# Latent attention in a two-layer hybrid trunk: queries one pair of heads ahead, the key latent normed between the first two pairs' queries, a fourth group of transposes on another bank

## The chip, the cores and the metric

The kernel runs on one core of one Trainium2 chip. The metric is the device time of one execution in microseconds, as the median over several runs.

## The reference

Two layers of a decoder trunk work on 512 tokens of width 1024 in float32. Each layer norms its input, projects it, sends it through three branches side by side (a state-space branch "SSD", latent attention "MLA", a gated delta rule "GDN"), merges them by gates and ends with a feed-forward block. The change touches the attention branch only:

```python
def mla_mixer(cq, ckv, k_rope, cos, sin, q_norm_g, w_uq, kv_norm_g, w_ukv):
    # H = 8 heads; cq is 512 wide, ckv 256; per head 128 + 64 (rotary) query columns
    q = (rmsnorm(cq, q_norm_g) @ w_uq).reshape(Bsz, S, H, MLA_NOPE + MLA_ROPE)
    q_nope, q_pe = jnp.split(q, [MLA_NOPE], axis=-1)
    q_pe = apply_rope(q_pe, cos[:, :, None, :], sin[:, :, None, :])
    kv = (rmsnorm(ckv, kv_norm_g) @ w_ukv).reshape(Bsz, S, H, MLA_NOPE + MLA_V)
    k_nope, v = jnp.split(kv, [MLA_NOPE], axis=-1)
    k_pe = apply_rope(k_rope, cos, sin)          # one rotary key for all heads
    ...
    # per block of 128 queries, causal:
    sc = q_nope @ k_nope + q_pe @ k_pe
    pr = jax.nn.softmax(sc * scale, axis=-1)
    out = pr @ v
```

## The kernel before

**Products.** Every float32 operand is split into a high part rounded to the matmul's format and a low remainder: ScalarE makes the high part (names ending in "h", or "hi"), VectorE the low part ("l", "lo"). A product is three matmuls into one accumulator, high by high (L181), low by high (L182 or L183), high by low (helper mm3, L179). A weight block is fetched by a transfer on SP's queue into "wraw" (two buffers), then split into "whi" (L159, ScalarE) and "wlo" (L160, VectorE). TensorE's accumulators live in eight banks: four named "acc" for projections, three named "sm" for small products, transposes and scores, one named "yt" that collects an attention head's output.

**Order.** The program is written in one order, and a scheduler decides ahead of time how the instructions of each engine stand behind each other, from dependencies, from priorities (`tc.high_priority`) and from when a buffer of a pool comes free. On the chip each engine takes its own list in that order and waits on semaphores of the others. A transfer inside the chip's memory that ScalarE issues (queue ACTq) stands in ScalarE's list as well.

**Attention before.** The two latents are in token-major tiles. The function `latent` squares and sums each (ScalarE), takes the power -1/2 (POOL), scales the rows (L495, VectorE), transposes in groups of four 128x128 blocks (L500, TensorE) into a bank, and splits the result with the gain (L260 ScalarE, L261 VectorE) into cqh, cql (four tiles each) or ckh, ckl (two each). The query latent has four such groups, for which there are three "sm" banks. Both latents are normed before any query is made. Then a loop over the four pairs of heads (hp, L540) does, in this order: the pair's query weights and 36 query matmuls from cqh and cql (three accumulators of 4 x 3 matmuls), the copies qh and ql (L568, L569), the scaled rotary part qp (L575); its rotation `rope`, which swaps halves by four transfers on ScalarE's queue (L513) and combines them on VectorE (L515 to L517); a second swap by two transfers (L580) so that either head has its half on the partitions it needs; the copies qps (L584, L586) and qpl (L585). Then the pair's keys and values: weights, 2 x 6 key matmuls, kh and kl; four value accumulators and vh, vl. Then for each of the two heads the scores of four row blocks, each from six matmuls (L617 to L622), the maximum (L626), the exponential (L629), the scaling, transposes of the probabilities (L639) and the product with v (L655 to L657) in the "yt" bank. Behind pair 0 the step sizes of the recurrent branches are called (`step_sizes`, L375 to L416); the scheduler moves much of them forward.

The kernel's start norms the layer's input in the same manner: row tiles scaled on VectorE (L291, by nrs from POOL, L265), transposed (L296), split into xh and xl (L261); the first products are with a narrow weight block into "yt" (L181 to L183 with mix as weights).

## Time and profile before

| | |
|---|---|
| median of 3 runs | 2350.89 us (2350.47 to 2352.99) |
| profiled execution | 2350.16 us |
| its span | 2348.4 us |
| granted TensorE clock | 0.999 |
| TensorE busy | 2307.8 us |
| VectorE busy | 1607.3 us |
| ScalarE busy | 1154.4 us |
| POOL busy | 58.5 us |

The profile is of one execution. "Busy" is the time in which an engine worked; it does not tell who waited for whom. The attention stage is short beside the whole: in layer 0 it runs from about 55 us to about 215 us, in layer 1 from about 1215 us to about 1365 us, with projections of other branches mixed in.

### The profile page before, as it was taken

The numbers are of one execution on the slowest core, as the hardware profiler recorded it, in microseconds if no ns is written. First come the engines' busy times: TensorE is split into PE (matmuls) and PEld (weight loads), VectorE is DVE, ScalarE is ACT, GpSimd is POOL, SyncE is SP. The second block draws the span as 40 slices with busy tenths as digits, with TensorE's granted clock in tenths as the row PEclk, the third lists the DMA queues.
The fourth block names the chain that finished last, engine by engine and source line by source line (L and its number), as shares of the span: only waits on it lengthen the run. The fifth ranks groups of instructions, "written<-read, shape, count | busy, mean of one in ns | idle before, by whom it ended". The sixth has DMA issues, their size and how long they took to land.

```text
span 2348.4 us, 32069 instructions
## 1 busy us (share of the span) xinstructions
PE 2307.8 (98%) x11972; PEld 1896.2 (81%) x11972; DVE 1607.3 (68%) x3184; ACT 1154.4 (49%) x2305; POOL 58.5 (2%) x76
## 2 busy tenths in 40 slices
PE   8999999999999999999999999999999999999998
PEld 7787788888887888888887887888887878888886
DVE  6776756775675458767757777667766645677668
ACT  5655434533453345545656553444334534555545
POOL 0000000000000000000000000000000000000000
PEclk9999999999999999999999999999999999999999
DMA  4322232252222443233132222323422224333231
GB/s 131 91 64 72 65 97 70 79 149 73 73 63 72 143 150 102 72 125 117 46 100 78 73 72 70 93 65 106 117 81 66 62 81 161 126 111 105 90 108 45
DMA packets 194172, 215.16 MB, mean 92 GB/s; under 512 B 32352, under 2 KB 153696, under 8 KB 194016
## 3 DMA queue, kind: packets, MB, share of 16 engines
q1 hardware_dynamic: 190496, 207.87, 29.1%
q10 hardware_dynamic: 3520, 5.25, 0.9%
q8 instruction: 94, 1.54, 0.3%
q14 instruction: 62, 0.51, 0.1%
HBM read 200.50 MB, written 7.34 MB: 89 GB/s over the span
## 4 chain that ended last, share of the span: by engine, by line
PE 90%; DVE 5%; DMA 2%; ACT 1%; POOL 1%; issue 1%; SPq 0%; ACTq 0%; DVEq 0%; POOLq 0%
PE acc L181 23%; PE acc L182 23%; PE acc L183 23%; PE sm L183 2%; PE sm L181 2%; PE sm L182 2%; PE sm L735 1%; DVE wlo L160 1%; PE sm L639 1%; PE yt L182 1%; PE yt L181 1%; PE yt L183 1%; PE sm L1000 1%; PE sm L296 1%; PE sm L461 1%
## 5 line engine op out<-in xcount | busy, mean ns | idle before, releaser
L160 DVE TENSOR_TENSOR wlo<-wraw,whi 128x512 fp32r<-128x512 f32 x552 | 377.9, 688 | 401.8 <-ACT whi L159 391.8
L159 ACT CAST whi<-wraw 128x512 fp32r<-128x512 f32 x552 | 341.9, 621 | 623.6 <-PE acc L182 407.9
L181 PE MATMUL acc<-xh,whi 128*128 128x512 f32 (+1 forms) x1184 | 462.0, 391 | 0.0
L182 PE MATMUL acc<-xl,whi 128*128 128x512 f32 (+1 forms) x1184 | 459.4, 388 | 0.0
L183 PE MATMUL acc<-xh,wlo 128*128 128x512 f32 (+1 forms) x1184 | 459.0, 388 | 0.0
L182 PEld LDWEIGHTS acc<-xl,whi 128*128 128x128 f32 x1184 | 223.0, 188 | 42.5 <-issue 1.0
L183 PEld LDWEIGHTS acc<-xh,wlo 128*128 128x128 f32 x1184 | 222.9, 188 | 41.8 <-issue 0.5
L181 PEld LDWEIGHTS acc<-xh,whi 128*128 128x128 f32 x1184 | 222.8, 189 | 41.7 <-issue 0.5
L181 PE MATMUL acc<-yh,whi 128*128 128x512 f32 x384 | 153.1, 402 | 0.0
L182 PE MATMUL acc<-yl,whi 128*128 128x512 f32 x384 | 152.3, 397 | 0.0
L183 PE MATMUL acc<-yh,wlo 128*128 128x512 f32 x384 | 151.4, 394 | 0.0
L183 PE MATMUL acc<-whi,xl 128*128 128x512 f32 (+1 forms) x384 | 144.0, 375 | 0.0
L181 PE MATMUL acc<-whi,xh 128*128 128x512 f32 (+1 forms) x384 | 143.9, 376 | 0.0
L182 PE MATMUL acc<-wlo,xh 128*128 128x512 f32 (+1 forms) x384 | 143.4, 373 | 0.0
L676 DVE SCALAR_TENSOR_TENSOR cva<-acc,pc,cva 128x511 f32<-128x511 f32 (+2 forms) x168 | 120.2, 743 | 16.7 <-ACT cva L672 9.5
L159 ACT CAST whi<-wr 128x512 fp32r<-128x512 f32 x128 | 79.5, 621 | 68.3 <-PE acc L183 32.7
L181 PE MATMUL acc<-whi,yh 128*128 128x512 f32 x256 | 99.7, 390 | 0.0
L183 PE MATMUL acc<-whi,yl 128*128 128x512 f32 x256 | 99.7, 389 | 0.0
L182 PE MATMUL acc<-wlo,yh 128*128 128x512 f32 x256 | 99.6, 389 | 0.0
L160 DVE TENSOR_TENSOR wlo<-wr,whi 128x512 fp32r<-128x512 f32 x128 | 85.8, 685 | 12.6 <-ACT whi L159 12.1
L182 PEld LDWEIGHTS acc<-yl,whi 128*128 128x128 f32 x384 | 72.2, 188 | 16.1 <-issue 1.9
L181 PEld LDWEIGHTS acc<-yh,whi 128*128 128x128 f32 x384 | 71.6, 188 | 16.8 <-ACT yh L260 2.3
(409 smaller groups left out, 4597.9 us busy)
## 6 DMA issues: line engine op xcount, KB each, us to landing
wraw<-in_w_in_dram SPq DMA_DIRECT2D x148, 512.0 KB, 3.6
wraw<-in_w_up_dram SPq DMA_DIRECT2D x64, 512.0 KB, 3.7
wr<-in_w_down_dram SPq DMA_DIRECT2D x32, 1024.0 KB, 5.0
wraw<-in_w_mla_out_dram SPq DMA_DIRECT2D x16, 512.0 KB, 3.4
wraw<-in_w_ssd_out_dram SPq DMA_DIRECT2D x16, 512.0 KB, 3.4
wraw<-in_w_gdn_out_dram SPq DMA_DIRECT2D x16, 512.0 KB, 3.3
wraw<-in_w_out_dram SPq DMA_DIRECT2D x16, 512.0 KB, 3.7
wraw<-in_mla_w_uq_dram SPq DMA_DIRECT2D x16, 384.0 KB, 3.4
```

Source lines behind the costliest of these rows:

```text
L159: act.copy(hi, raw)
L160: dve.tensor_tensor(lo, raw, f32(hi), ALU.subtract)
L181: pe.matmul(o, ah, bh, start=start, stop=False, skip_group_check=more)
L182: pe.matmul(o, ah, bl, start=False, stop=False, skip_group_check=more)
L183: pe.matmul(o, al, bh, start=False, stop=stop, skip_group_check=more)
L296: pe.transpose(ps[:, j * P : (j + 1) * P], xr[j % 2][:, kk * P : (kk + 1) * P], ident)
L461: pe.matmul(ps, w, cum[1][:, t].rearrange("p i l -> p (i l)"), start=True, stop=True)
L639: pe.transpose(ps[:, n : n + P], pn[t][:, kb * P : (kb + 1) * P], ident)
L676: dve.scalar_tensor_tensor(acc[:, d:], ps[:, : S - d], taps_[3 - d], acc[:, d:], ALU.mult, ALU.add)
L735: pe.matmul(py[:, h * 64 : (h + 1) * 64], e2[h // 4][:, h % 4, :], xd[:, h * 64 : (h + 1) * 64], start=True, stop=True)
L1000: pe.matmul(po[:, h * P : (h + 1) * P], pt_[:, h, :], vn[:, h * P : (h + 1) * P], start=True, stop=True)
```

## The change

It has three parts. (1) In `latent`, the fourth group of transposes (k == 3, query latent only) is written to the "yt" bank instead of an "sm" bank. (2) The loop's body is cut into three functions, `queries(hp)`, `keys(hp)` and `attend(hp, ...)`. The order is now: queries of pair 0, norm of the key latent, queries of pair 1; then for each pair its keys and values, its scores and output, and behind pairs 0 and 1 the queries of the pair after next. (3) Since two pairs' queries are alive at once, the odd pairs' qh, ql, qps and qpl lie in tiles that others use later (the output tiles "y", two of the query latent's tiles), and the half of qpl that must be zero is cleared anew on POOL (`clean`, eight memsets more). The lines of the loop move: the swap transfers L513 and L580 of before are L512 and L585 after, the qps copies L584 and L586 are L594 and L596, the scores L617 to L622 are L634 to L639, qh is written in L548 and qp in L580.

```diff
@@ latent
             for k in range(nk):
-                ps = sm_bank()
+                ps = y_bank() if k == 3 else sm_bank()
@@
         cqh, cql = latent(cq_tok, 512, g_q, "cq")
-        ckh, ckl = latent(ck_tok, 256, g_kv, "ck")
...
-        qpl = [mk(ml, [P, S], F32R, f"qpl{j}") for j in range(2)]
+        base_qpl = [mk(ml, [P, S], F32R, f"qpl{j}") for j in range(2)]
+        clean = lambda x, j: pool.memset(f32(x[64 * (1 - j) : 64 * (1 - j) + 64]), 0.0)
         for j in range(2):
-            pool.memset(f32(qpl[j][64 * (1 - j) : 64 * (1 - j) + 64]), 0.0)
+            clean(base_qpl[j], j)
...
-        for hp in range(4):
+        y_home = lambda k: [mk(lp, [P, S], F32R, f"y{e}{k}") for e in "hl"]
+        cq_home = lambda k: [mk(ml, [P, S], F32R, f"cq{e}{k}") for e in "hl"]
+        def queries(hp):
...
-            qs = head_tiles(pq, "q", scale)
+            qs = head_tiles(pq, "q", scale, [y_home(hp * 2 + j if hp == 1 else 6 + j) for j in range(2)] if hp % 2 else None)
...
-            qps = [mk(ml, [P, S], F32R, f"qps{j}") for j in range(2)]
+            if hp % 2:
+                qps, qpl = zip(*((y_home if hp == 1 else cq_home)(k) for k in ((4, 5) if hp == 1 else (2, 3))))
+                for j in range(2):
+                    clean(qpl[j], j)
+            else:
+                qps, qpl = [mk(ml, [P, S], F32R, f"qps{j}") for j in range(2)], base_qpl
...
+            return qs, qps, qpl
+        def keys(hp):
...
+            return ks, vs
+        def attend(hp, qs, qps, qpl, ks, vs):
...
+        qq = [queries(0)]
+        ckh, ckl = latent(ck_tok, 256, g_kv, "ck")
+        qq.append(queries(1))
+        for hp in range(4):
+            attend(hp, *qq[hp], *keys(hp))
+            if hp < 2:
+                qq.append(queries(hp + 2))
             if hp == 0:
                 dec, ndec, beta, dtq, dsk, g24 = step_sizes()
```

How the instructions stand on the engines moves at three places of layer 0. The first is TensorE's list where the query latent's last transposes meet the first query matmuls; "ct" is the identity, "mix" the scaled latent, acc_725 to acc_727 the three accumulators of pair 0. Before:

```order
L500 MATMUL sm_652<-ct_75,mix_224 128x128
L181 MATMUL acc_725<-cqh_120_630,whi_730 128x512
L181 MATMUL acc_726<-cqh_120_630,whi_730 128x512
L181 MATMUL acc_727<-cqh_120_630,whi_730 128x512
L500 MATMUL sm_659<-ct_75,mix_221 128x128
L500 MATMUL sm_659<-ct_75,mix_222 128x128
L500 MATMUL sm_659<-ct_75,mix_223 128x128
L500 MATMUL sm_659<-ct_75,mix_224 128x128
L182 MATMUL acc_725<-cql_124_634,whi_730 128x512
```

The same place in the changed kernel, where pair 0's accumulators are acc_691 to acc_693:

```order
L500 MATMUL sm_652<-ct_75,mix_224 128x128
L500 MATMUL yt_659<-ct_75,mix_221 128x128
L500 MATMUL yt_659<-ct_75,mix_222 128x128
L500 MATMUL yt_659<-ct_75,mix_223 128x128
L500 MATMUL yt_659<-ct_75,mix_224 128x128
L181 MATMUL acc_691<-cqh_120_630,whi_696 128x512
L181 MATMUL acc_692<-cqh_120_630,whi_696 128x512
L182 MATMUL acc_691<-cql_124_634,whi_696 128x512
```

The transposes have moved ahead of all query matmuls, and two query matmuls instead of three now stand ahead of the first one that reads cql.

The second place is ScalarE's list around the copies kh of pair 0's keys. Before:

```order
L568 ACTIVATE qh_792<-acc_725 128x512
L568 ACTIVATE qh_796<-acc_726 128x512
L552 CAST whi_1140<-wraw_1138 128x256
L553 CAST whi_1140<-wraw_1138 128x128
L552 CAST whi_1155<-wraw_1138 128x256
L256 CAST kh_846<-acc_832 128x512
L553 CAST whi_1155<-wraw_1138 128x128
L575 ACTIVATE qp_800<-acc_727 128x512
L513 DMA mix_802<-qp_800 32x512
L256 CAST kh_850<-acc_833 128x512
```

In the changed kernel mix_773 is pair 0's rotated part, mix_777 its swapped form, whi_925 and whi_929 the key weights, acc_822 the first query accumulator of pair 1:

```order
L585 DMA mix_777<-mix_773 64x512 x2
L594 CAST qps_162_780<-mix_773 64x512
L159 CAST whi_925<-wraw_923 128x512
L159 CAST whi_929<-wraw_923 128x512
L594 CAST qps_163_781<-mix_773 64x512
L596 CAST qps_162_780<-mix_777 64x512
L596 CAST qps_163_781<-mix_777 64x512
L256 CAST kh_947<-acc_933 128x512
L548 ACTIVATE yh_189_889<-acc_822 128x512
```

kh stood ahead of pair 0's swap transfers and now stands behind them and behind the four qps copies. On TensorE the readers of kh follow the first key accumulator at once (acc_934 is the second):

```order
L183 MATMUL acc_933<-ckh_171_805,wlo_930 128x512
L634 MATMUL sm_1003<-kh_947,qh_758 128x256
L634 MATMUL sm_1017<-kh_947,qh_758 128x256
L634 MATMUL sm_1031<-kh_947,qh_758 128x384
L181 MATMUL acc_934<-ckh_170_804,whi_925 128x512
```

Before, the second key accumulator and value matmuls stood between the first key accumulator and the first score matmul; now nothing does.

The third place is VectorE's list at the program's start; nrs_279 is the norm factor of the fourth row tile, xr_283 that tile scaled, xl_31 the first low part of the normed input. Before:

```order
L264 TENSOR_SCALAR nrs_279<-nrs_279 128x1
L261 SCALAR_TENSOR_TENSOR xl_31_130<-sm_150,pc_104,xh_23_122 128x256
L261 SCALAR_TENSOR_TENSOR xl_33_132<-sm_159,pc_104,xh_25_124 128x256
L160 TENSOR_TENSOR mix_189<-wraw_186,mix_188 128x384
L261 SCALAR_TENSOR_TENSOR xl_32_131<-sm_150,pc_104,xh_24_123 128x256
L160 TENSOR_TENSOR mix_193<-wraw_186,mix_192 128x384
```

In the changed kernel:

```order
L264 TENSOR_SCALAR nrs_279<-nrs_279 128x1
L291 TENSOR_SCALAR xr_283<-h_89,nrs_279 128x1024
L160 TENSOR_TENSOR mix_189<-wraw_186,mix_188 128x384
L261 SCALAR_TENSOR_TENSOR xl_31_130<-sm_150,pc_104,xh_23_122 128x256
L160 TENSOR_TENSOR mix_193<-wraw_186,mix_192 128x384
L261 SCALAR_TENSOR_TENSOR xl_33_132<-sm_159,pc_104,xh_25_124 128x256
```

The scaling of the fourth row tile and one weight subtraction have moved ahead of the first xl.

More of the change, by code (lines that the diff above doesn't have):

```diff
@@ L532, in hybrid_kernel, with head_tiles @@
             pool.memset(f32(x[:, :P]), 0.0)
-        qpl = [mk(ml, [P, S], F32R, f"qpl{j}") for j in range(2)]
+        base_qpl = [mk(ml, [P, S], F32R, f"qpl{j}") for j in range(2)]
+        clean = lambda x, j: pool.memset(f32(x[64 * (1 - j) : 64 * (1 - j) + 64]), 0.0)
         for j in range(2):
-            pool.memset(f32(qpl[j][64 * (1 - j) : 64 * (1 - j) + 64]), 0.0)
+            clean(base_qpl[j], j)
         scale = (128 + 64) ** -0.5
         yh, yl = [None] * KD, [None] * KD
-        for hp in range(4):
+        def head_tiles(pss, nm, c=None, homes=None):
+            res = []
+            for j, ps in enumerate(pss):
+                hi, lo = homes[j] if homes else (mk(ml, [P, S], F32R, nm + e, 3) for e in "hl")
+                if c is None:
+                    split_act(hi, lo, ps)
+                else:
+                    act.mul(hi, ps, c)
+                    dve.scalar_tensor_tensor(lo, ps, c, f32(hi), ALU.mult, ALU.subtract)
+                res.append((hi, lo))
+            return res
+        y_home = lambda k: [mk(lp, [P, S], F32R, f"y{e}{k}") for e in "hl"]
+        cq_home = lambda k: [mk(ml, [P, S], F32R, f"cq{e}{k}") for e in "hl"]
+        def queries(hp):
             def q_weights():
@@ L558, in hybrid_kernel @@
             *pq, pp = dense_F(q_weights(), tiles(384), 512, cqh, cql)
-            def head_tiles(pss, nm, c=None):
-                res = []
-                for ps in pss:
-                    hi = mk(ml, [P, S], F32R, nm + "h", 3)
-                    lo = mk(ml, [P, S], F32R, nm + "l", 3)
-                    if c is None:
-                        split_act(hi, lo, ps)
-                    else:
-                        act.mul(hi, ps, c)
-                        dve.scalar_tensor_tensor(lo, ps, c, f32(hi), ALU.mult, ALU.subtract)
-                    res.append((hi, lo))
-                return res
-            qs = head_tiles(pq, "q", scale)
+            qs = head_tiles(pq, "q", scale, [y_home(hp * 2 + j if hp == 1 else 6 + j) for j in range(2)] if hp % 2 else None)
             qp = mk(ml, [P, S], F32, "qp")
@@ L580, in hybrid_kernel @@
                 act.dma_start(qd[64 * i : 64 * i + 64], qr[64 * (1 - i) : 64 * (1 - i) + 64])
-            qps = [mk(ml, [P, S], F32R, f"qps{j}") for j in range(2)]
+            if hp % 2:
+                qps, qpl = zip(*((y_home if hp == 1 else cq_home)(k) for k in ((4, 5) if hp == 1 else (2, 3))))
+                for j in range(2):
+                    clean(qpl[j], j)
+            else:
+                qps, qpl = [mk(ml, [P, S], F32R, f"qps{j}") for j in range(2)], base_qpl
             for j in range(2):
```

## The prediction

> **What bounds the kernel now.** I read the page first, for the span, the engines' shares and the chain that ended last. Row by row these are the span, the busy times and the chain by engine:

> ```profile
> span 2348.4 us, 32069 instructions
> PE 2307.8 (98%) x11972; PEld 1896.2 (81%) x11972; DVE 1607.3 (68%) x3184; ACT 1154.4 (49%) x2305; POOL 58.5 (2%) x76
> PE 90%; DVE 5%; DMA 2%; ACT 1%; POOL 1%; issue 1%; SPq 0%; ACTq 0%; DVEq 0%; POOLq 0%
> ```

> TensorE is busy for 98% of the span and is on the chain for 90% of it. The change leaves the number of TensorE's operations as it is, so only the time in which TensorE stands still can change. I therefore asked next for TensorE's waits (engine, waiting line, releaser: total us, times, longest):

> ```profile
> PE sm L620 <- ACT qps L586: 3.2, 3, 1.9
> PE acc L181 <- DVE vl L257: 2.2, 3, 0.8
> PE sm L500 <- DVE mix L495: 1.9, 2, 1.0
> PE sm L500 <- DVE cql L261: 1.2, 1, 1.2
> PE acc L181 <- ACT cqh L260: 0.6, 2, 0.3
> PE yt L656 <- DVE mix L257: 0.4, 2, 0.2
> ```

> These six are all of the attention stage, over both layers, and they add up to 9.5 us, 0.4% of the span. That is the most visible idle time that the change can take away. Everything that decides is therefore a matter of a microsecond at a place, and I went on to the timeline, TensorE's rows (start, duration, operation, in brackets the idle time before and its releaser):

> ```profile
> 60.24 0.98 PE L181 MATMUL acc<-cqh,whi 128*128 128x512 f32 x3 [0.29 <-ACT cqh L260]
> 62.43 0.66 PE L500 MATMUL sm<-ct,mix 128*128 128x128 f32 x4 [1.21 <-DVE cql L261]
> 66.36 0.63 PE L500 MATMUL sm<-ct,mix 128*128 128x128 f32 x4 [0.95 <-DVE mix L495]
> 80.19 0.47 PE L181 MATMUL acc<-cqh,whi 128*128 128x512 f32 x1 [0.65 <-DVE vl L257]
> 80.49 0.40 PE L182 MATMUL acc<-cql,whi 128*128 128x512 f32 x1
> 80.72 0.39 PE L183 MATMUL acc<-cqh,wlo 128*128 128x512 f32 x1
> 147.49 0.38 PE L620 MATMUL sm<-kps,qps 128*128 128x256 f32 x1 [0.78 <-ACT qps L586]
> 1278.83 0.39 PE L620 MATMUL sm<-kps,qps 128*128 128x256 f32 x1 [1.85 <-ACT qps L586]
> ```

> The second row is the query latent's last group of transposes, the third the key latent's first; the pair 80.49 and 80.72 gives what a 512-column matmul costs when it does not wait, 0.23 us from start to start. A difference of 0.2% (4.7 us) is about what a measurement of this kernel can tell from no change.

> **Part one, the transposes and the latents.** Before, the fourth group of transposes (62.43) waits for the first "sm" bank, which VectorE's cql copy empties. In the new order it writes the free "yt" bank and runs straight behind the third group. But the three query matmuls that stood ahead of it need cqh alone, and now only two of them do so before the first one that reads cql. VectorE's rows there:

> ```profile
> 61.01 0.26 DVE L402 SCALAR_TENSOR_TENSOR g<-spl,aexp 128x96 f32<-128x96 f32 x1
> 61.63 2.06 DVE L261 SCALAR_TENSOR_TENSOR cql<-sm,pc,cqh 128x512 fp32r<-128x512 f32 x3
> ```

> VectorE has the step-size chain of the recurrent branch ahead of cql until 61.6 and writes the first cql about 62.3 (a third of the 2.06 us that three take, behind 61.63). TensorE reaches it at about 61.1: the wait of 1.21 comes back as one of about 1.2 on the next matmul in layer 0. What is gained there is the four transposes moved into the hole, 4 x 0.11 us (0.63 for four with the tail of the last), say 0.35. In layer 1 that wait does not exist before (the row above has 1 time). The key latent's wait for L495 (0.95 in layer 0, 1.9 over both) goes: its transposes now stand behind 36 query matmuls, 36 x 0.23 = 8.3 us, and the squares, POOL's power and the scaling lie below that cover. If the cover were gone it would cost the 0.95 again. Gain: 1.9 + 2 x 0.35 = **2.6 us**, bounds 1.9 and 3.7 (all of L495, cql and cqh).

> **Part two, queries one pair ahead.** Pairs 1 and 2 no longer wait for qps (3.2), since their rotary halves are made one pair earlier; the accumulators that waited for the vl copies (2.2) now follow other work; and the two yt waits (0.4) have queries standing between. Gain **5.8 us**, bounds 3 and 5.8.

> What is late next is the first pair. In the new order three score matmuls of pair 0 stand right behind the first key accumulator, and on ScalarE the copy kh that they read stands behind both swap transfers of pair 0, four qps copies and two weight casts. Two of the qps copies wait for the swap to land. Before, kh stood ahead of all that. ScalarE's rows of before (ACTq is its sequencer issuing a transfer):

> ```profile
> 74.78 0.60 ACT L575 ACTIVATE qp<-acc 128x512 f32<-128x512 f32 x1
> 75.41 0.51 ACTq L513 DMA_DIRECT2D mix<-qp  x1
> 75.97 0.59 ACT L256 CAST kh<-acc 128x512 fp32r<-128x512 f32 x1 [0.59 <-PE acc L183]
> 81.78 0.50 ACTq L580 DMA_DIRECT2D mix<-mix  x1
> 82.76 0.54 ACTq L580 DMA_DIRECT2D mix<-mix  x1
> 85.62 1.27 ACT L586 CAST qps<-mix 64x512 fp32r<-64x512 f32 x2
> ```

> From qp to the first swap transfer is 81.78 - 74.78 = 7.0 us, and nothing in between is taken away. In the new order qp's last matmul is the 36th behind 62.3, so qp comes at about 70.7, and the swaps go out at about 77.7 and 78.3. How long a swap takes, from the view of line L580 and from the transfers issued between 111.7 and 112.3 us:

> ```profile
> DMA to landing us min/median/max: 2.2/2.3/5.6
> wraw<-in_mla_w_uq_dram SPq DMA_DIRECT2D x1, 384.0 KB, 3.9
> mix<-mix ACTq DMA_DIRECT2D x2, 128.0 KB, 3.3
> ```

> Alone it lands in 2.3 us; beside a weight load the two of 111 us average 3.3, and the slowest takes 5.6. Alone: landed 80.6, two copies of 1.27 together 81.9, kh 0.6 more, 82.5. TensorE gets there after 36 query matmuls, 8 transposes, 36 more query matmuls and 6 key matmuls: 62.3 + 78 x 0.23 + 8 x 0.11 = 81.1. So the wait is 1.2 to 1.4; with a landing of 4.3, 2.0 us longer. The weight load of pair 2 is released by pair 1's casts, at about the same 77.7, so the meeting is possible, not certain. I take 1.2, ends 0 and 4.5 (a landing of 5.6).

> Behind it, the second key accumulator takes the bank of pair 1's first query, which is emptied by a ScalarE copy right behind kh and a VectorE subtraction: 82.5 + 0.6 + 0.6 = 83.7 against 82.8 for TensorE (kh plus three score matmuls), 0.85, ends 0 and 1.2. Two query weights of pair 1 are cast behind rope transfers that hold the sequencer 0.5 us each: 0.45 and 0.25, ends 0 and 1.2 together. Two more places have the kind of wait of the rows above: the last pair's first key accumulator waits for a bank that vl copies empty (nearest row 0.65; here the queue on VectorE is longer by a normalisation: 1.15, ends 0.65 and 1.85), and head 1 of pair 2 has its exponentials behind pair 3's qps copies (nearest rows 0.78 and 1.85; I take 0.7, as the transfer is issued earlier, ends 0 and 1.85). 0.1 is left for the same thing at pair 0. Loss in one layer: 1.2 + 0.85 + 0.7 + 1.15 + 0.7 + 0.1 = 4.7, in both **9.4 us**.

> The eight memsets more go to POOL, busy 2% of the span, on tiles read much later: nothing, and 0.5 each at most if a qpl write came first. SP's issues are the same in number.

> **Part three, the program's start.** The scheduler places it anew: VectorE now has the fourth row tile's scaling (L291) and a weight subtraction ahead of the first xl. Rows of POOL, VectorE and TensorE of before:

> ```profile
> 13.41 0.55 POOL L265 TENSOR_TENSOR nrs<-nrs,nhalf 128x1 f32<-128x1 f32 x1 [1.12 <-DVE nrs L264]
> 13.25 0.88 DVE L261 SCALAR_TENSOR_TENSOR xl<-sm,pc,xh 128x256 fp32r<-128x256 f32 x2
> 14.04 0.55 DVE L160 TENSOR_TENSOR mix<-wraw,mix 128x384 fp32r<-128x384 f32 x1
> 17.75 0.74 DVE L291 TENSOR_SCALAR xr<-h,nrs 128x1024 f32<-128x1024 f32 x1
> 14.29 0.41 PE L182 MATMUL yt<-xl,mix 128*96 128x256 f32 x1
> 18.39 0.63 PE L182 MATMUL acc<-wlo,xh 128*128 128x512 f32 x1
> 18.81 0.52 PE L183 MATMUL acc<-whi,xl 128*128 128x512 f32 x1
> 19.17 0.39 PE L181 MATMUL acc<-whi,xh 128*128 128x512 f32 x1
> 19.40 0.39 PE L182 MATMUL acc<-wlo,xh 128*128 128x512 f32 x1
> ```

> POOL is done at 13.96; the scaling ends at 14.7, the subtraction at about 15.2, the first xl at 15.6 instead of 13.7. TensorE's row of 14.29 starts 1.3 us later. Some is given back, since 17.75 no longer stands ahead of the later transposes: I take **0.85** lost, ends 0.3 and 1.5, once. The same rows bear on the clock: up to 18.81 a 512-column matmul takes 0.42 from start to start, from 19.17 on 0.23. [...] In terms of rows: were the rate change to come 1.3 us later, 1.3 x (0.42 - 0.23) / 0.42 = 0.6 us more, which I hold inside the ends.

> **The sum.** -2.6 - 5.8 + 9.4 + 0.85 = +1.85 us. The profiled execution took 2350.16 us (1.76 outside the span), which gives 2352.0; the median of three is 0.73 above it, so 2352.7. I forecast **2352.5 us**, within 0.2%.

> **Rivals.** *The covers hold (faster).* The swap lands alone, ScalarE gets kh out before TensorE needs it, and only the start and some 1 us of the new waits are left: -8.4 + 0.85 + 1 = -6.5, 2344.3 us. For it: the median of the sixteen landings is 2.3 us, and the time from qp to the swap was measured with key and value copies in between that now come later; were it 5.8 instead of 7.0 us, kh would be there in time. Against it: the 5.8 would have to hold in both layers, and kh's place in ScalarE's order leaves it no slack at 7.0. 0.23.

> *ScalarE's order holds kh behind a slow swap (slower).* The swap of pair 0 meets the load of pair 2's weights in both layers. It decides from a landing above 3.3 us; at 4.3 the first wait is 3.2 instead of 1.2 in each layer, and the exponentials that stand behind pair 1's and pair 3's qps copies take a third of the same lateness, 0.65 each: 1.85 + 2 x (2.0 + 1.3) = +8.5, 2359.3 us. For it: 3.3 as the mean beside a load, 5.6 as the slowest; against it: the load's start hangs on pair 1's casts, which may be a microsecond later. [...] 0.30.

> *Waits only change places* is the forecast itself: 0.47. That the change doesn't do what it says is excluded for the order of work, which moves as described.

> **How the numbers follow.** Within 0.2% is 2346.2 to 2355.6. The forecast case's own range is 2347 to 2357: its terms' ends are far apart but do not all go one way. To hold 8 in 10 the range takes in the centre of both rivals: low 2342.5, high 2360. Faster 0.23, same 0.47, slower 0.30.

> **What would show it.** In the changed kernel's trace: no wait of L500 for mix or of the score lines for qps; a cql wait of about 1.2 in layer 0 only; a wait of about 1.2 of the first score matmul (now L634) for kh, with 0.85 at the next accumulator; the first yt matmul with xl at about 15.6. If the swap (now L585) lands above 4 us, the slower rival holds; if L634 doesn't wait for kh at all, the faster one does. It is wrong as a whole if TensorE's idle time in the attention stages changes by more than 5 us, or if time moves outside the start and these stages, for instance where layer 1's order moves with it.

## The result, and the profile after

| | before | changed |
|---|---|---|
| median of 7 runs | 2350.89 us | 2358.03 us |
| lowest to highest | 2350.47 to 2352.99 | 2355.34 to 2362.46 |
| granted TensorE clock, by run | 0.999 (profiled run) | 0.998, 0.998, 0.998, 0.997, 0.997, 0.996, 0.995, from the shortest run to the longest |
| profiled execution | 2350.16 us | 2355.34 us |

The ratio is 1.0029, 95% interval 1.0018 to 1.0041: slower by 7.1 us. The range of the prediction holds that; its likeliest case, no more than 0.2% either way, did not come. What came is the rival with kh held behind a slow swap, which had a chance of 0.30 and 2359.3 us, though not by all of its prices.

The page of the changed kernel gives the span and the engines as before, and a TensorE that is as busy as ever:

```profile
span 2353.5 us, 32071 instructions
PE 2308.2 (98%) x11972; PEld 1896.8 (81%) x11972; DVE 1607.5 (68%) x3184; ACT 1154.7 (49%) x2305; POOL 62.6 (3%) x84
PE 89%; DVE 5%; DMA 2%; ACT 2%; issue 1%; POOL 1%; SPq 0%; ACTq 0%; DVEq 0%; POOLq 0%
```

So TensorE was given no more work. Its waits (engine, line, releaser: us, times, longest), of the places that matter here:

```profile
PE sm L634 <- ACT kh L256: 4.3, 2, 2.2
PE acc L181 <- DVE vl L257: 2.8, 2, 1.4
...
PE yt L182 <- DVE xl L261: 1.7, 1, 1.7
PE sm L656 <- DVE pn L648: 1.7, 2, 0.8
PE acc L182 <- DVE cql L261: 1.5, 1, 1.5
...
PE sm L917 <- issue: 1.1, 2, 0.8
PE yt L672 <- ACT mix L256: 1.1, 1, 1.1
...
PE acc L181 <- ACT whi L572: 0.8, 2, 0.4
...
PE acc L181 <- ACT whi L159: 0.4, 1, 0.4
```

The six waits of before are gone or changed: none for qps, none for the key latent's scaled rows, and of the list above 12.6 us belong to the attention stages, against 9.5 before. The largest is new: 4.3 us for kh, once in each layer. ScalarE's rows in front of it in layer 0 show why (L585 is the swap, L594 and L596 the qps copies):

```profile
78.20 1.15 ACTq L585 DMA_DIRECT2D mix<-mix  x2
79.39 0.62 ACT L594 CAST qps<-mix 64x512 fp32r<-64x512 f32 x1 [2.63 <-DVE wlo L574]
80.45 1.14 ACT L159 CAST whi<-wraw 128x512 fp32r<-128x512 f32 x2 [0.44 <-DMA wraw<-in_mla_w_ukv_dram]
81.62 0.62 ACT L594 CAST qps<-mix 64x512 fp32r<-64x512 f32 x1
83.35 1.26 ACT L596 CAST qps<-mix 64x512 fp32r<-64x512 f32 x2 [1.12 <-DMA mix<-mix]
84.51 0.57 ACT L256 CAST kh<-acc 128x512 fp32r<-128x512 f32 x1
```

ScalarE stands idle for 1.12 us in front of the copies that read the swapped tile, with kh behind them. The slowest landing from the view of L585 is this stage's: the two of 78 us took 3.6 and 4.6 us, beside two weight loads.

```profile
DMA to landing us min/median/max: 2.2/2.8/4.6
```

Then TensorE's rows of the same place in layer 1, and what follows it:

```profile
1247.44 0.69 PE L634 MATMUL sm<-kh,qh 128*128 128x256 f32 x3 [2.21 <-ACT kh L256]
1248.16 0.80 PE L181 MATMUL acc<-ckh,whi 128*128 128x512 f32 x1
1248.76 0.63 PE L182 MATMUL acc<-ckl,whi 128*128 128x512 f32 x1
1249.19 0.63 PE L183 MATMUL acc<-ckh,wlo 128*128 128x512 f32 x1
1249.61 0.63 PE L181 MATMUL acc<-ckh,whi 128*128 128x512 f32 x1
1250.04 0.63 PE L182 MATMUL acc<-ckl,whi 128*128 128x512 f32 x1
```

After the pause the matmuls stand at 0.43 us from start to start, where 0.23 is usual. The table of stretches (from:to, length, busy us and count of PE, PEld, DVE, ACT, POOL, then the granted clock, DMA share, GB/s) has the clock itself:

```profile
1244.00:1247.40 3.40, 1.23 (x5) 0.67 (x4) 1.26 (x2) 2.13 (x5) 0.00 (x0) 1.00 0.65 183
1247.40:1250.80 3.40, 3.33 (x9) 2.56 (x10) 2.82 (x5) 1.74 (x4) 0.00 (x0) 0.58 0.10 27
```

TensorE worked for 1.23 of 3.40 us, and in the next 3.40 us the clock was 0.58. In layer 0 the pause of 2.10 us was followed by nothing of the kind. So there are two candidates for the 7 us: waiting, of which the profiled execution shows 4.3 us at kh, and a clock that differs from run to run.

### The profile page after: what moved, and what is told of

The parts are those of the page before. It is cut to its first block, busy times and chain, and to the rows that moved or that the text cites. A ratio compares the mean times of both kernels' runs of the same rounds, so it can differ in the third digit from the quotient of the medians.

```text
span 2353.5 us, 32071 instructions
## 1 busy us (share of the span) xinstructions
PE 2308.2 (98%) x11972; PEld 1896.8 (81%) x11972; DVE 1607.5 (68%) x3184; ACT 1154.7 (49%) x2305; POOL 62.6 (3%) x84
## 4 chain that ended last, share of the span: by engine, by line
PE 89%; DVE 5%; DMA 2%; ACT 2%; issue 1%; POOL 1%; SPq 0%; ACTq 0%; DVEq 0%; POOLq 0%
PE acc L181 22%; PE acc L182 22%; PE acc L183 22%; PE sm L181 2%; PE sm L182 2%; PE sm L183 2%; PE sm L760 1%; DVE wlo L160 1%; DMA mix<-mix 1%; PE sm L656 1%; PE yt L182 1%; PE yt L181 1%; PE sm L1025 1%; PE yt L183 1%; PE sm L461 1%
## 5 line engine op out<-in xcount | busy, mean ns | idle before, releaser
L160 DVE TENSOR_TENSOR wlo<-wraw,whi 128x512 fp32r<-128x512 f32 x552 | 377.7, 688 | 395.1 <-ACT whi L159 388.3
L159 ACT CAST whi<-wraw 128x512 fp32r<-128x512 f32 x552 | 341.5, 621 | 607.5 <-PE acc L182 394.5
L181 PE MATMUL acc<-xh,whi 128*128 128x512 f32 (+1 forms) x1184 | 462.6, 392 | 0.0
L182 PE MATMUL acc<-xl,whi 128*128 128x512 f32 (+1 forms) x1184 | 459.3, 388 | 0.0
L183 PE MATMUL acc<-xh,wlo 128*128 128x512 f32 (+1 forms) x1184 | 458.9, 388 | 0.0
L182 PEld LDWEIGHTS acc<-xl,whi 128*128 128x128 f32 x1184 | 223.2, 189 | 42.3 <-issue 1.0
L183 PEld LDWEIGHTS acc<-xh,wlo 128*128 128x128 f32 x1184 | 222.8, 188 | 42.2 <-issue 0.5
L181 PEld LDWEIGHTS acc<-xh,whi 128*128 128x128 f32 x1184 | 222.7, 188 | 41.5 <-issue 0.5
L181 PE MATMUL acc<-yh,whi 128*128 128x512 f32 x384 | 153.0, 402 | 0.0
L182 PE MATMUL acc<-yl,whi 128*128 128x512 f32 x384 | 152.3, 397 | 0.0
L183 PE MATMUL acc<-yh,wlo 128*128 128x512 f32 x384 | 151.4, 394 | 0.0
L183 PE MATMUL acc<-whi,xl 128*128 128x512 f32 (+1 forms) x384 | 144.5, 377 | 0.0
L181 PE MATMUL acc<-whi,xh 128*128 128x512 f32 (+1 forms) x384 | 143.9, 377 | 0.0
L182 PE MATMUL acc<-wlo,xh 128*128 128x512 f32 (+1 forms) x384 | 143.6, 374 | 0.0
L159 ACT CAST whi<-wr 128x512 fp32r<-128x512 f32 x128 | 79.5, 621 | 68.3 <-PE acc L183 32.7
L181 PE MATMUL acc<-whi,yh 128*128 128x512 f32 x256 | 99.7, 389 | 0.0
L183 PE MATMUL acc<-whi,yl 128*128 128x512 f32 x256 | 99.7, 389 | 0.0
L182 PE MATMUL acc<-wlo,yh 128*128 128x512 f32 x256 | 99.6, 389 | 0.0
L160 DVE TENSOR_TENSOR wlo<-wr,whi 128x512 fp32r<-128x512 f32 x128 | 85.8, 686 | 12.4 <-ACT whi L159 11.7
L181 PEld LDWEIGHTS acc<-yh,whi 128*128 128x128 f32 x384 | 71.6, 188 | 16.8 <-ACT yh L260 2.3
L182 PEld LDWEIGHTS acc<-yl,whi 128*128 128x128 f32 x384 | 72.2, 188 | 16.0 <-issue 1.9
## 6 DMA issues: line engine op xcount, KB each, us to landing
wraw<-in_mla_w_uq_dram SPq DMA_DIRECT2D x16, 384.0 KB, 3.4
```

What stands on the lines that cost most here:

```text
L159: act.copy(hi, raw)
L160: dve.tensor_tensor(lo, raw, f32(hi), ALU.subtract)
L181: pe.matmul(o, ah, bh, start=start, stop=False, skip_group_check=more)
L182: pe.matmul(o, ah, bl, start=False, stop=False, skip_group_check=more)
L183: pe.matmul(o, al, bh, start=False, stop=stop, skip_group_check=more)
```

## The experiments

The theory after this first look: kh behind the landing swap costs its waiting, and its pause costs half-rate time besides. Rivals: the start's 1.5 us; the clock having a cause of its own; new waits that simply take the place of any one that is removed. Medians are of 5 to 11 runs; each ratio is to runs of the kernel before on the same chip (medians 2350.0 to 2351.0 us there).

**The start taken back.** The two memsets of pair 1's zero halves had been hoisted ahead of POOL's first norm factor. Without them VectorE's list at the start is that of before.

```diff
-                    clean(qpl[j], j)
...
+                    dve.tensor_scalar(qpl[j][other], qr[other], 0.0, None, ALU.mult)
```

> The changed kernel with one thing taken back: the odd pairs' zero halves of qpl are written by VectorE from the rotated query (times 0), so that no memset is hoisted to the program's start and VectorE's list at the start is that of the kernel before. Theory: two memsets ahead of POOL's first norm factor are what moved the start, and its wait of 1.7 us for the first xl goes: 1.5 us less than the changed kernel, 2356.5 us, with the wait for kh (2.1 and 2.2 us) unchanged and the scatter of the times as wide as that of the changed kernel. Rival: the start is hidden (the first input's transfer decides), then 2358.0 as the changed kernel.

Measured: 2359.01 us, ratio 1.0031 (1.0019 to 1.0044), clock 0.997 in all five runs. The wait for xl at the start is gone, but kh's waits are 5.3 us instead of 4.3. The theory's gain of 1.5 us didn't come. VectorE's zeroing could be to blame, so the zeros are made on POOL instead:

```diff
-                    clean(qpl[j], j)
...
+                    pool.tensor_tensor(qpl[j][other], qr[other], qr[other], ALU.subtract)
```

> The changed kernel with the start taken back without work for VectorE: the odd pairs' zero halves are made on POOL as the rotated query minus itself, which can't be hoisted. The run before it, which made them on VectorE, gained 1.9 us at the start (counted from the first matmul) and lost it again in the attention stage. Theory: the loss there came from the zeroing on VectorE; without it the start's 1.5 to 1.9 us stay gained: 2356 us, with kh's waits of 2.1 to 2.9 us left and the clock at about 0.997. Rival: the start has no part in the time, 2358.

Measured: 2359.94 us, 1.0032 (1.0019 to 1.0045). Again nothing, and VectorE isn't the reason. TensorE's row at kh in layer 0:

```profile
84.17 1.12 PE L635 MATMUL sm<-kh,qh 128*128 128x256 f32 x3 [3.08 <-ACT kh L256]
85.08 0.63 PE L181 MATMUL acc<-ckh,whi 128*128 128x512 f32 x1
85.51 0.63 PE L182 MATMUL acc<-ckl,whi 128*128 128x512 f32 x1
```

3.08 us instead of 2.10: of the 1.5 us that TensorE gained at the start it waited for 1.0 at kh, and here the half rate follows in layer 0. In layer 1 the wait is 2.6 us instead of 2.2.

**kh ahead of the landing.** Pair 0's qps and qpl copies are written behind its keys, so that kh and the second kh come first on ScalarE.

```diff
-                act.copy(qps[j][half], qr[half])
-                ...
+            def turn():
+                ...
+            if hp > 0:
+                turn()
+            return qs, qps, qpl, turn
...
+            if hp == 0:          # in attend, behind keys(0)
+                turn()
```

> The changed kernel with pair 0's qps and qpl copies written behind its keys, so that on ScalarE kh no longer stands behind the copies that wait for the swap to land. The start stays as changed. Theory: the wait for kh is the largest loss (2 x 2.1 idle, 2 x 2.3 from start to start) and also what lowers the clock: its pause of over 2 us is followed in layer 1 by 2.6 us at half rate. Then 4.6 us of waiting and some 2 us of half rate go: about 2351.5 us, clock 0.999 in every run, and a scatter of under 3 us. Rival one: a new wait takes its place (qps for the next score lines, acc banks), 2356 us or more. Rival two: the lower clock has nothing to do with the wait, then 2353.5 us and times as scattered as before (7 us).

Measured: 2352.25 us (2350.34 to 2355.95), 1.0007 (0.9999 to 1.0016); clock 0.999 in nine of eleven runs. As the theory had it, kh isn't waited for any more, the clock is back, and by the medians 5.8 us of the 7.1 are gone (5.2 by the ratios). Some waits have come up in its place:

```profile
PE acc L181 <- DVE vl L257: 2.9, 4, 1.2
...
PE acc L181 <- ACT whi L571: 1.6, 2, 0.8
...
PE acc L182 <- DVE cql L261: 1.5, 1, 1.5
...
PE acc L183 <- DVE wlo L573: 1.3, 2, 0.6
...
PE acc L181 <- ACT whi L572: 1.2, 2, 0.8
PE sm L639 <- ACT pn L651: 1.2, 2, 0.7
```

They sum to 9.7 us, and to 10.2 with two of 0.3 and 0.2 that are not shown, against the 12.6 of the changed kernel: waiting in the attention stages accounts for 2.4 of the 5.2 to 5.8 us. That the lower clock made the rest is argued, not shown. The profiled execution of this kernel was one of its slowest (2355.46 us) and that of the changed kernel its fastest (2355.34 us), so two executions that took the same time are compared here, and their rows can't split the difference of the medians. What the two traces do show is that the 3.41 us at half rate in layer 1 are gone. The scatter, 5.6 us, is wider than the 3 expected. With the start taken back too (by VectorE, and by POOL):

> Both edits together. If the two losses are independent: 1.5 us below the run with kh alone, about 2350 us, the same as the kernel before. If the start's pause is what scatters the clock, this one is steady and the run with kh alone isn't.

> The same start, and pair 0's qps copies behind its keys. Theory: no pause over 1.6 us is left in the attention stages, the clock reads 0.999 in every run, and the time is 1.5 to 1.9 us below the run with kh alone (2352.3): 2350.5 us, no better and no worse than the kernel before. Rival (the start is worth nothing): 2352.3.

Measured: 2354.89 us, 1.0014 (1.0005 to 1.0023), with clocks from 0.996 to 0.999; and 2353.13 us, 1.0009 (1.0000 to 1.0018), with 0.999 in all eleven runs. The first has a new pause, scores waiting for the exponentials, 2.0 us at the longest, and half rate behind it in both layers (clock 0.996 in that execution); the second has not, and is steady. The wait of the first:

```profile
PE sm L640 <- ACT pn L652: 3.7, 2, 2.0
```

The start therefore is worth nothing that a run's total shows, with kh's wait or without.

**kh still later.** In the first start run, kh is made twice:

```diff
+                    if late and j == 0:
+                        with tc.high_priority(30):
+                            for _ in range(1):
+                                act.copy(hi, ps)
                     split_act(hi, lo, ps)
```

> The run with the start taken back, and in it the copy kh of pair 0's first head made twice on ScalarE, with one other copy between: kh is ready about 1.07 us later in both layers, and TensorE's pause there grows from 2.1 to about 3.2 us. If only waiting counts: 2 x 1.07 less what the following wait for the bank gives back (up to 0.3 each): 1.6 to 2.1 us above the run with the start taken back. If a longer pause drops the clock more often (a half-rate stretch of about 2.6 to 3.4 us costs 1.3 to 1.7 us): up to 3 us more than that, 2 to 5 us above, with a clock of 0.997 or less in most runs.

Measured: 2359.65 us, 1.0039 (1.0025 to 1.0052), clock 0.996 to 0.997. The waits for kh grew from 5.3 to 7.4 us, as meant, the median by 0.64 us only. The intervals of the two runs overlap widely; this run decides nothing on the size.

**Pauses by themselves.** Behind the end of the kernel before, bursts of matmuls alternate with chains of copies on ScalarE.

```diff
+    for n in PAUSES:             # second run: for n, m in PAUSES, with m matmuls
+        ps = acc_bank()
+        for _ in range(24):
+            pe.matmul(ps, w, z, start=True, stop=True)
+        for i in range(n):
+            y = mk(lp, [P, S], F32R, "mix", 8)
+            act.copy(y, ps if i == 0 else f32(z))
+            z = y
```

> The kernel before with a row of 96 bursts behind its end: 24 matmuls of 512 columns (5.4 us), then TensorE waits for a chain of 1 to 6 copies on ScalarE, in turn 1, 2, 3, 4, 5, 6, sixteen times. The pauses are about 0.9 to 4 us. This tells nothing of the kernel's time (some 700 us are added). If a pause lowers the clock: behind pauses of under about 1.5 us all matmuls keep 0.23 us from start to start, behind some of those of 1.6 to 3 us and nearly all over 3.4 us they stand at 0.43 for 2 to 3.4 us, at a share that rises with the pause. If the half rate seen in layer 1 has another cause: 0.23 everywhere.

> The row of bursts behind the kernel before once more, with pauses of 1.3, 2.0, 2.6 and 3.3 us (2 to 5 copies), 24 of each, and bursts of 24 to 38 matmuls, so that the pauses fall anywhere in a cycle of 3.41 us. In the first row every round of six pauses took about 54.6 us, 16 cycles of 3.41 us, so each kind of pause met the same point of the cycle each time. If a fixed cycle decides by how much of it stood idle: 1.3 us never drops the clock, 2.0 us in some half of the cases, 2.6 in three quarters, 3.3 in nearly all, and the end of the half rate falls on the same point of the cycle each time. If the length of the pause alone decides: 0 of 24 at 1.3 and 24 of 24 at 2.0 and above, as in the first row.

The first gave, by the length of the pause: at 0.67 and 1.32 us none of 16, at 1.97 us and above all of them (16, 16, 16, and 15 of 15). That looked like a threshold in length, but a round of the six pauses took 54.6 us, 16 times the 3.41 us for which the granted clock of the changed kernel stands at 0.50 (1247.96 to 1251.38 us), so each kind of pause met the same point of a cycle of that length. The second, TensorE's rows (a row is one burst: start, length of the burst, count, the pause before it):

```profile
2367.59 5.96 PE L1258 MATMUL acc<-mix,whi 128*128 128x512 f32 x25 [1.97 <-ACT mix L1261]
...
2425.82 7.19 PE L1258 MATMUL acc<-mix,whi 128*128 128x512 f32 x24 [3.27 <-ACT mix L1261]
...
2477.52 5.78 PE L1258 MATMUL acc<-mix,whi 128*128 128x512 f32 x24 [1.32 <-ACT mix L1261]
...
2526.82 7.35 PE L1258 MATMUL acc<-mix,whi 128*128 128x512 f32 x24 [1.97 <-ACT mix L1261]
```

24 matmuls take 5.78 us behind a pause of 1.32. Behind a pause of 1.97 they take 7.35 us in one case, and in another 25 take 5.96. Counted over all bursts, with the loss against 0.227 us per matmul (0.1 to 0.2 us in bursts without half rate):

| pause | followed by half rate | loss where it is |
|---|---|---|
| 1.3 us | 0 of 24 | |
| 1.97 us | 10 of 24 | 1.70 to 1.78 us |
| 2.62 us | 16 of 24 | 1.46 to 1.75 us |
| 3.27 us | 20 of 23 | 1.51 to 2.98 us |

In thirteen of the 46 the loss is 1.46 to 1.66 or 2.69 to 2.98 us: such a burst began at half rate, and its length, with 0.427 us per matmul before the return to the full rate and 0.227 behind it, tells where the return lies. These thirteen returns, from 2428.9 to 3183.3 us, fall within 0.05 us of one point of a cycle of 3.413 us, the length that fits them best of all from 1.5 to 8 us. Counted from that point, the ten pauses of 1.97 us that were followed by half rate began at 0.25 to 1.46 us, the other fourteen at 1.53 to 3.22 us. So the pause's place in a cycle that the bursts don't shift decides, and how much of the cycle stood idle fits the shares (expected were none, half, three quarters and nearly all). What makes the cycle was not measured.

The same cycle tells why only one of the changed kernel's two pauses at kh was followed by half rate. Its drop came at 1247.96 us; counted back from there in steps of 3.413 us, a cycle ends at 84.01, in the middle of layer 0's pause. Its table of stretches, cut at the cycle's ends (the first two are layer 0, the third is layer 1 up to the drop):

```profile
80.60:84.01 3.41, 2.06 (x7) 0.97 (x6) 2.11 (x4) 2.24 (x5) 0.00 (x0) 1.00 0.64 166
84.01:87.42 3.41, 2.23 (x10) 1.71 (x11) 2.30 (x4) 2.83 (x6) 0.00 (x0) 1.00 0.28 95
1244.55:1247.96 3.41, 1.20 (x6) 0.61 (x5) 1.25 (x3) 2.29 (x5) 0.00 (x0) 1.00 0.51 129
```

In layer 0 the pause of 2.10 us was shared out, and TensorE was busy for 2.06 and 2.23 us of the two cycles; in layer 1 the pause of 2.21 us fell within one, with 1.20 us busy. In one case two shorter pauses did together what one does: in the first run with kh first and the start taken back, a cycle with 1.50 us busy was followed by half rate in layer 0, and its waits were one of 1.62 us, most of it in that cycle, and one of 0.38 us:

```profile
90.69:94.10 3.41, 1.50 (x6) 0.99 (x7) 3.32 (x10) 3.34 (x11) 0.00 (x0) 0.99 0.14 31
```

The point at which the idle share of a cycle becomes enough was not measured. The bursts place the 1.5, 1.6 and 3.4 us that the expectations name no closer than this: half rate in 0 of 24 cases at 1.32 us, 10 of 24 at 1.97, 20 of 23 at 3.27.

**The change's parts.** The line on the fourth transposes alone, in the kernel before:

> The kernel before with the one line on the fourth group of transposes: to the free bank. Theory: its wait of 1.21 us becomes a wait of the next matmul for cql, and only the transposes' own 0.35 us in each layer are gained: 0.7 us, not to be told from the kernel before (2350.3). Rival: the line brings the whole 1.2 us in layer 0 and shifts the rest of the stage: 2349 or less.

Measured: 2353.73 us, 1.0015 (1.0006 to 1.0023). Not neutral, slower by 3.6 us, and its waits say how:

```profile
PE sm L620 <- ACT qps L586: 5.5, 4, 2.0
...
PE acc L182 <- DVE cql L261: 1.5, 1, 1.5
```

The wait for cql came back at the next matmul, as expected; but the waits for qps rose from 3.2 to 5.5 us, two of them 2.0 us long. Others fell, so that all waits of the attention stages sum to 10.4 us against 9.5. Behind the longest, in layer 1, the granted clock stands at 0.50 for 3.41 us, which costs up to 1.7 us more. Together that is at most 2.6 of the 3.6 us; the rest isn't accounted for. Then the latents as changed, but with each pair's queries made only behind the scores of the pair before (`qq.append(queries(hp + 1))` behind `attend`, start as before):

> Start as before, fourth transposes to the free bank and the key latent normed behind pair 0's queries as in the change, but queries not ahead: pair hp+1's queries behind pair hp's scores. It keeps the gain of part one (1.9 us of the key latent's wait, and 0.7) and has the qps waits of the kernel before (3.2) and its waits for vl (2.2) back. Theory (part one is a gain, part two is the loss): 2.6 us below the kernel before, 2348.3 us, clock 0.999. Rival (part one has its own loss, the cql wait of 1.5 in layer 0): 2351.

Measured: 2362.56 us, 1.0049 (1.0035 to 1.0063), the worst of all, clock 0.996 to 0.997:

```profile
PE acc L181 <- DVE vl L257: 5.5, 2, 2.9
PE sm L638 <- ACT qps L597: 3.4, 2, 1.9
...
PE acc L181 <- DVE cql L257: 2.6, 2, 1.3
PE acc L182 <- DVE ckl L261: 2.0, 2, 1.3
```

With the key latent normed late, pair 0's keys have no queries to mix with any more, and its matmuls run ahead of ckl and of the v copies. My expectation was wrong by 14 us: part one is no gain by itself, it needs the queries ahead as cover.

**Two tries at a faster version.** The query weights' casts at high priority (in the run with kh first and the POOL start):

```diff
+                        with tc.high_priority():
+                            act.copy(nv(hi), rv[:, :, :P])
+                            ...
```

> The run with pair 0's qps copies behind its keys and the start as before, and besides the query weights' casts at high priority, as those of all other weights are. In that run TensorE waits 0.8 us in each layer for the cast of pair 2's first weight (L571) and 1.5 for its remainder (L573). Theory: both waits go, up to 4.6 us: 2348.5 us, faster than the kernel before by some 2 us, clock 0.999. Rival: ahead of all else in ScalarE's and VectorE's lists, the casts hold up the rope transfers or kh themselves and bring a new pause: 2353 or more, with a lower clock if the pause passes 1.6 us.

Measured: 2357.94 us, 1.0030 (1.0018 to 1.0041). The rival: the waits for L571 and L573 are gone, and vl is waited for instead, 2.6 us at the longest and 2.4 at the same place of the other layer, with the clock at 0.997 to 0.998:

```profile
PE acc L181 <- DVE vl L257: 7.9, 6, 2.6
```

Last, the change's own order, with the copies that wait for the swap on POOL (the start is taken back by POOL here too):

```diff
-                act.copy(qps[j][other], qd[other])
+                pool.tensor_copy(qps[j][other], qd[other])
```

> The changed kernel with its start as before, and the qps copies that wait for the swap moved from ScalarE to POOL (busy under 3% of the span); the order of the program is otherwise that of the change. ScalarE then never stands behind a landing transfer. Theory: kh comes when its accumulator is done, some 0.6 us behind TensorE's arrival instead of 2.6 to 3.1, the exponentials of the later pairs are no longer held either, no pause passes 1.6 us, the clock reads 0.999: 2350 us, level with the kernel before, 2348.5 if the start's 1.5 us show at last. [...]

Measured: 2354.58 us, 1.0019 (1.0010 to 1.0028), clock 0.999 in ten of eleven runs. The wait for kh falls to 0.83 us a layer, and the clock returns, with the program written in the change's own order: it was ScalarE's list, held by the landing, that made the pause. Against the same kernel with the copies on ScalarE (2359.94 us, 1.0032) it gains 5.4 us by the medians and 3.1 by the ratios, whose intervals overlap. The total is not the 2350 us that was expected, though: by the medians 4.6 us more than the kernel before are left. New waits for pn have come up:

```profile
PE sm L657 <- DVE pn L649: 2.7, 5, 0.7
PE sm L657 <- ACT pn L647: 2.2, 2, 1.1
...
PE sm L635 <- ACT kh L256: 1.7, 2, 0.8
```

The copies themselves take 0.60 to 1.10 us on POOL (min/median/max in ns; the rows differ by the tile written):

```profile
L597 POOL CAST qps<-mix x8: 610/624/1089, 82.9 to 1287.6; 64x512 fp32r<-64x512 f32 x8
L597 POOL CAST yh<-mix x4: 652/967/1039, 94.5 to 1259.8; 64x512 fp32r<-64x512 f32 x4
L597 POOL CAST cqh<-mix x4: 604/634/1100, 153.8 to 1318.7; 64x512 fp32r<-64x512 f32 x4
```

None of the versions beats the kernel before.

## Why the prediction was right or wrong, step by step

*What bounds the kernel, and what goes.* Right. The waits for qps and for the key latent are gone; the cql wait of layer 0 came back at the next matmul, 1.46 us where 1.2 was worked out, and none of that length in layer 1.

*kh behind the swap.* The mechanism was right, to the row: kh stands behind L596, which waits for the landing. The failing term is its size. I took a landing of 2.3 us and a wait of 1.2; the swaps were sent at 78.20 and 78.74, where 77.7 and 78.3 were worked out, and landed 3.6 and 4.6 us later, beside weight loads; the later of pair 0's two landed 4.4 to 5.2 us after its issue in both layers of the changed kernel and of nine experiments; the run with the query weights at high priority is the exception, with 2.4. That a weight load makes a landing late is seen by neighbourhood only, and the load's time matters: with the queries not ahead, the first swap of layer 0 landed in 2.28 us and the second, sent 0.04 us before a load of 512 KB, in 4.86; in the exception the swaps were sent 1.8 and 2.3 us behind such a load, and it didn't delay them. The waits were 2.10 and 2.21 us, 4.3 together where the sum had 2.4. I had called the meeting possible, not certain, and taken the uncollided value.

*The second key accumulator.* 0.85 us was wrong: TensorE's starts show 0.2 there. *The other waits.* Two query weight casts 0.45 and 0.25: one is waited for, 0.44 and 0.33 us; the other isn't. A wait of 0.39 us in layer 0 for the key weights' cast (L159) was not in the sum. The last pair's key accumulator 1.15: 1.41 in each layer. The exponentials 0.7: 0.83 and 0.84, though by the profile VectorE's scaling, behind the exponentials, comes last. Not in the sum: 1.1 us in layer 1 for a tile of transposed probabilities (L672).

*The start.* The delay was there: 1.72 us of waiting for the first xl, and counted from the first matmul the start was 1.5 us longer, the upper end of what I gave. But it is worth nothing in the total by two pairs of runs. With kh's wait this is accounted for: 1.0 us of it came back there. Without kh's wait (2352.25 and 2353.13 us) it is open why. The profiles show a part: the waits in the attention stages are 10.7 us with the start taken back and 10.2 without, with 1.6 more for a weight's remainder (L573). The first matmul came at 8.7 to 11.5 us in the profiles, whatever the kernel, and that scatter is as large as the effect.

*The sum.* In the attention stages the waits rose by 12.6 - 9.5 = 3.1 us where 9.4 - 8.4 = 1.0 was forecast. With 1.6 more at the start (1.7 for xl and 0.2 for the narrow weights, against 0.3), 1.1 at L917 and 1.2 of half rate (six spacings of 0.2), less 1.0 by which the first transpose came earlier (at 9.29 instead of 10.25 us), this makes 6.0; the profiled execution is longer by 5.18, so 0.8 too much is counted somewhere.

*The clock.* This is the step that was missing. I weighed the half rate for the start alone and priced every other pause at its own length. A pause of 2.1 to 2.2 us lies between the rows with 10 of 24 and 16 of 24: about half, by an estimate from them; by that estimate two such pauses make one drop of 1.7 us in an execution on average. The profiled execution had one. All 34 runs of the six kernels with a pause of over 2.1 us in these stages (the changed one, both starts, the later kh, the queries not ahead, the query weights) read 0.995 to 0.998; the 33 runs of the three whose longest pause there is 1.5 us (the two with kh first and no new pause, the copies on POOL) read 0.999 in 30. With pauses of 2.0 us both occur. The kernel before has one pause of 1.85 us and reads 0.999, seldom 0.998. The pauses are those of the one execution of each kernel that was profiled. The changed kernel's scatter has the size that the clock gives: from its shortest run to its longest the reading falls from 0.998 to 0.995, which over 2355 us is 7.1 us, and the times differ by 7.1 us (a reading is rounded to 0.001, or 2.4 us). But one stretch of 3.41 us at 0.50 lowers the mean by 0.0007 only, so the run at 0.995 must hold at least three stretches more than the profiled one, and two pauses with one drop each don't give them. The traces of other runs show two stretches in a row at about 83 us, in layer 0 (6.83 us, in three experiments) and one at the program's start (in one); where the stretches of the slowest runs lay is not on record.

*L917.* In the delta-rule branch TensorE stood 1.1 us in a burst of 32x32 matmuls, released by nothing that the profile shows. It is 0.2 to 1.9 us in the profiles of the changed kernel and its variants, and not there in the kernel before; what moves it was not tried, and stays open. It lies outside the start and the attention stages, and time moving there was one of the prediction's own signs of being wrong as a whole; it is 1.1 of the 5.18 us.

*The faster rival* fell with kh. *The slower rival* named the place, the collision and the point from which it decides (3.3 us; measured 4.4 and 4.6 for the later swap). Its +8.5 us were made of waits alone; of the 7.1 that came, waits are about half, by the profiled execution, and that the clock made the rest is argued from its readings. The lateness of the exponentials that it priced at 0.65 each did not come: they were waited for 0.83 and 0.84 us, where the forecast itself had 0.7. That the range held the measured time is owed to this rival, whose centre it took in.

## What to carry to other kernels

Read in an order listing which copies stand behind a copy that waits for a transfer: an engine that takes its list in order hands a late landing to everything behind it (here 2.10 and 2.21 us of waiting for kh). Here that told more than the sum of all idle times. Where such a transfer is sent at the moment a weight load is released, price it at the landing that was seen beside a load (here 3.6 to 5.2 us), not at the median (2.3 us in the kernel before). A TensorE pause of 1.97 us cost 1.7 us beyond its length in 10 of 24 cases, by where it fell in a cycle of 3.41 us, and two pauses that shared a cycle counted together in one case; one of 1.3 us by itself cost nothing more in 24. A scatter of the granted clock between runs is a reason to look for such a pause.
